# A second gate branch by seven products of quarters, and low parts of weights by accumulating transfers, in a hybrid decoder layer

## The chip, the cores and the metric

The kernel runs on one core of one Trainium2 chip. The metric is the time of one launch on the device in microseconds (us). Three runs of the kernel before gave a median of 1034.51 us (1033.88 to 1037.33). The engines of a core work side by side, each through its own instruction list in order: TensorE (PE) multiplies matrices, VectorE (DVE), ScalarE (ACT) and GpSimd (POOL) work elementwise, SyncE (SP) only issues transfers (DMAs). An instruction that waits holds back everything behind it on its own engine.

## The reference

One pre-norm layer over 512 tokens of width 1024, in float32. A normed input `u` goes through one wide projection `w_in`. Its columns feed three token mixers (attention in three dilated groups, multi-scale pooling, a chunked state space scan) and three gates:

```python
u = rmsnorm(x, ln1_g[i])
proj = u @ w_in[i]
q, k, v, pool_in, z, xbc, dt_raw, gate_pre = jnp.split(proj, split_idx, axis=-1)
...
y_b = pool_mixer(pool_in, pool_w[i], pool_scale[i]) @ w_b[i]
...
gates = jax.nn.sigmoid(gate_pre + b_gate[i]).reshape(b, s, N_BRANCH, D_MODEL)
merged = gates[:, :, 0] * y_a + gates[:, :, 1] * y_b + gates[:, :, 2] * y_c
x = x + merged @ w_o[i]
x = x + conv_ffn(rmsnorm(x, ln2_g[i]), ffn_w_up[i], ffn_conv_w[i], ffn_conv_b[i], ffn_w_down[i])
```

The change concerns `gates[:, :, 1]`, a product of `u` (512 x 1024) with 1024 columns of `w_in`, and how some weights are split.

## The kernel before

**Three products for one.** PE multiplies in a reduced format. Every float32 operand is split into a high part (rounded) and a low part (what rounding left). A product is the sum of three: high x high, high x low, low x high. `uh` and `ul` hold the parts of `u`, transposed, so that the 1024 inputs lie on partitions in 8 blocks of 128. A weight block goes through a `Job`: `fetch` (L184) loads it into `raw` (pool `wraw`, 2 buffers), `cast` (L196) rounds it on ACT into `wh` (3 buffers) in two halves, `lows` (L216) subtracts on DVE into `wl` (2 buffers), and the job's body runs the matmuls (`mm3`, L235) and hands the PSUM tile (pool tag `mm`, 4 buffers) to an evacuation.

**The order of the work** is written out by hand. `program()` yields the jobs in order, and the engine lists of PE, ACT, DVE and POOL are exactly the order in which the instructions are emitted. Before the body of job n the main loop emits `prepare`: the low part of job n+1, the cast of job n+2 (its two halves put off to the next two `step`s), the fetch of job n+3. So on ACT the casts for job n+2 stand behind the evacuations of job n, and the low part of job n+2 comes after both casts. `job.form` makes a weight by a subtraction on DVE at the cast, `job.then` subtracts after the low part. `wraw` has two buffers, so a fetch waits until the low part that reads the buffer's earlier content is done.

**Fillers.** `step()` advances everything in `running` and takes one more item from `waiting`: `attend(g)` queues the attention of one group as items (scores on PE, bias and maximum on DVE, exponentials on ACT, then two steps later transposes on PE, L769), `ssd_prep`, and so on. A job steps once per column chunk. With a chunk in `more` it runs as `chunk_a2`, which does the three products over the first four blocks, steps, and then does the other four.

**Seven products for eight.** `sevens` (L341) and `qk_sevens` (L647) compute a projection as a 2 x 2 block product by 7 products of quarters instead of 8. `sums_of_u` (L400) makes the sums of quarters of `u` that this takes, `side_u` hands them out, and two quarters of the weight wait in `ypool` (tag `xs`, 2 buffers, which later hold the SSD input). In `qk_sevens` a weight quarter of 128 columns is loaded into PE and 256 tokens of `u` move through it.

**Around the change** the order before is: `pool_out_job`; `branch_jobs(1, w_b, ...)`, 4 jobs of two column chunks that make `MG`, with the attention of group 0 as filler; the gates of the second branch, chunks 0 to 3 (`gate_jobs(1, 0, SPLIT)`, L1146); seven jobs for the values of groups 1 and 2 (`v_pair`); seven for the queries and keys of group 1; `attend(1)`; gate chunks 4 to 7; 6 jobs of the SSD input (`xbc_evac`, L900 and L904); `ssd_start`. A gate chunk is 24 matmuls of 512 columns. Its evacuation is a sigmoid on ACT and a product with `MG` on DVE (L1148).

Of the kernel before, what the change touches and what calls it, by code (L numbers as in the profile page):

```python
# [10 lines left out]
F32 = mybir.dt.float32  # L11
F32R = mybir.dt.float32r
AF = mybir.ActivationFunctionType
OP = mybir.AluOpType
# [58 lines left out]
class Job:  # L73


    def __init__(self, parts, k, c, body):
        self.parts, self.k, self.c, self.body = parts, k, c, body
        self.raw = self.split = None
        self.late = self.short = False
        self.load = self.form = self.then = None  # L80


@with_exitstack
def trunk(ctx: ExitStack, tc, out, x, rel_bias, ln1_g, w_in, b_gate, w_a, pool_w, pool_scale, w_b,
# [80 lines left out]
    def after(n, it):  # L165
        for _ in range(n):
            yield
        yield from it
# [40 lines left out]
    def lows(job, cuts=1, eng=None):  # L209

        w, h = job.c // cuts, job.high
        l = wlp.tile([P, job.k, job.c], F32R, name="wl", tag="wl")
        job.split = h, l
        for i in range(cuts):
            o = slice(i * w, (i + 1) * w)
            (eng or dve).tensor_tensor(l[:, :, o], job.raw[:, :, o], h[:, :, o].bitcast(F32),  # L216
                                       OP.subtract)
            yield

    def low(job, cuts=1, eng=None):  # L220
        for _ in lows(job, cuts, eng):
            pass
        if job.then:
            job.then()

# [174 lines left out]
    def sums_of_u(p):  # L400

        f = []
        for k in (2 * p, 2 * p + 1):
            f.append(T("uf"))
            dve.tensor_tensor(f[-1], uh[:, k, :].bitcast(F32), ul[:, k, :].bitcast(F32), OP.add)
        yield
        yield from sums_of(*f, T("sah", F32R), T("sal", F32R),
                           lambda j, h, l: US.__setitem__((j, p), (h, l)))
# [733 lines left out]
    def gate_jobs(b, lo=0, hi=8):  # L1142
# [6 lines left out]

        return jobs_a(w_in, C_GATE + b * D + lo * P, hi - lo, uhk, ulk, KD, evac)  # L1150

    def branch_jobs(b, w, parts, nk, last=False, more=()):
        def evac(m, ps):
            if b == 1:
                MG[m] = T("yo")
                act.copy(MG[m], ps)
                return
            s = SG[b, m]
            dve.tensor_tensor(s, s, ps, OP.mult)
            (dve if last else pool).tensor_tensor(MG[m], MG[m], s, OP.add)  # L1160
            if last:
                h, l = T("mgh", F32R), T("mgl", F32R)
                act.copy(h, MG[m])
                dve.tensor_sub(l, MG[m], h.bitcast(F32))
                MH[m] = (h, l)

        return jobs_a(w, 0, 8, lambda k: parts[k][0], lambda k: parts[k][1], nk, evac,
                      width=256 if nk > 4 else 512, more=more)
# [273 lines left out]
    def program():  # L1442
# [4 lines left out]
        yield from pool_out_job()  # L1447
        yield Call(lambda: attend(0))
        yield Call(lambda: waiting.insert(3, ssd_prep()))
        for i, job in enumerate(branch_jobs(1, w_b, YB, 8, more=range(7))):  # L1450
            if i == 3:
                yield Call(lambda: running.extend(after(p, sums_of_u(p)) for p in range(4)))
            yield job
        load, pair = v_pair()
        yield Call(load)
        yield from gate_jobs(1, 0, SPLIT)
        loads, qk = qk_sevens(1)
        for i, job in enumerate(pair):
            yield job
            if i == 4:  # L1460
                yield Call(loads)
        yield from qk
        yield Call(lambda: attend(1))
        yield from gate_jobs(1, SPLIT)
        yield from jobs_a(w_in, C_XBC, 12, uhk, ulk, KD, xbc_evac)
        yield Call(ssd_start)
        yield from qk_jobs(2)
        yield Call(lambda: attend(2))
# [215 lines left out]
NBIG = 54  # L1684
MORE = 2
AT = ((9, 10, 11, 12, 13, 14, 15), (17, 17, 18, 19, 20, 21, 22))
SPLIT = 4
MIX = "ZZ0zz1ggggaa"
SSD_ORDER = ((0, 0, 1), (1, 0, 1), (0, 1, 1), (2, 0, 1), (1, 1, 1), (3, 0, 1), (2, 1, 1), (3, 1, 1))
WARM = 12  # L1690
# [29 lines left out]
```

## Time and profile before

| what | value |
|---|---|
| median of 3 runs | 1034.51 us |
| time of the profiled execution | 1034.33 us |
| its span in the profile | 1032.0 us |
| PE busy | 99% of the span |
| ACT, DVE, POOL busy | 48%, 69%, 13% |
| mean granted clock of TensorE | 0.999 |

What lies outside the span is 1034.33 - 1032.0 = 2.3 us. A sum that is made on the span is carried to the time of the run with that difference unchanged. In the views below, a row of the timeline gives start, length, engine, line, operation, output <- input and count. A row of the groups gives count, busy time, mean ns of one, and the idle time before it with what ended it.

### The profile page before, as it was taken

Reading aid. Unit: us, or ns where it says so; the run is one execution under the profiler, and the core shown is the slowest. Engines: PE = TensorE matmul, PEld = TensorE weight load, DVE = VectorE, ACT = ScalarE, POOL = GpSimd, SP = SyncE. Lnnn points to the kernel's source line nnn. Section 1 sums busy time; section 2 is a strip of 40 time slices with the busy share of each in tenths; the row PEclk is TensorE's granted clock in tenths of the full one; section 3 lists DMA queues with packets and bytes.
Section 4 is the critical chain, followed back from the end, with each engine's and each line's share of the span. In section 5 each row is a group of like instructions: output and inputs, shape, how many; then the busy total and the mean of one; then the engine's idle time right before and its main releaser. Section 6 shows DMA issues by size and latency. Waiting matters only on the chain.

```text
span 1032.0 us, 13285 instructions
## 1 busy us (share of the span) xinstructions
PE 1021.4 (99%) x5276; PEld 858.8 (83%) x5276; DVE 714.3 (69%) x948; ACT 498.7 (48%) x800; POOL 133.5 (13%) x114
## 2 busy tenths in 40 slices
PE   9999999999999999999999999999999999999997
PEld 8998877899888887788888888898888888888885
DVE  6553566788756648666688856767778759876776
ACT  6432545454674363567575324545445544445334
POOL 1770000000000001100044501101111100111002
PEclk9999999999999999999999999999999999999999
DMA  8444312134322364551253625543231233412222
GB/s 256 148 128 139 107 57 75 31 88 137 123 82 82 94 155 110 132 144 45 79 157 121 202 82 205 175 143 114 82 123 41 85 119 98 148 41 82 82 82 82
DMA packets 112300, 115.52 MB, mean 112 GB/s; under 512 B 5203, under 2 KB 97174, under 8 KB 112239
## 3 DMA queue, kind: packets, MB, share of 16 engines
q1 hardware_dynamic: 111647, 113.83, 36.1%
q8 instruction: 41, 0.67, 0.3%
q10 hardware_dynamic: 592, 0.86, 0.2%
q14 instruction: 20, 0.16, 0.0%
HBM read 110.87 MB, written 2.22 MB: 110 GB/s over the span
## 4 chain that ended last, share of the span: by engine, by line
PE 90%; DVE 5%; ACT 3%; issue 1%; DMA 1%; ACTq 0%; DVEq 0%
PE pa L235 30%; PE pu L235 22%; PE pb L235 12%; PE pd L235 7%; PE pqk L235 6%; PE pa L1571 2%; PE pq L235 2%; PE pu L1375 1%; PE ps L740 1%; PE pt L769 1%; PE ppw L235 1%; PE po L781 1%; DVE wl L216 1%; DVE xs L1130 1%; PE py L1054 1%
## 5 line engine op out<-in xcount | busy, mean ns | idle before, releaser
L216 DVE TENSOR_TENSOR wl<-raw,wh 128x2048 fp32r<-128x2048 f32 (+3 forms) x93 | 213.5, 2297 | 47.8 <-ACT wh L196 42.7
L196 ACT CAST wh<-raw 128x1024 fp32r<-128x1024 f32 (+3 forms) x184 | 183.6, 1017 | 40.9 <-DMA raw<-in_ffn_w_down_dram 13.2
L1248 DVE SCALAR_TENSOR_TENSOR hc<-pu,fcol,hc 128x510 f32<-128x510 f32 x88 | 65.8, 748 | 48.4 <-ACT hc L1245 46.8
L235 PE MATMUL pa<-uh,wh 128*128 128x512 f32 x384 | 98.4, 398 | 0.0
L235 PE MATMUL pa<-ul,wh 128*128 128x512 f32 x384 | 94.9, 389 | 0.0
L235 PE MATMUL pa<-uh,wl 128*128 128x512 f32 x384 | 94.8, 389 | 0.0
L235 PEld LDWEIGHTS pa<-ul,wh 128*128 128x128 f32 x384 | 72.1, 188 | 15.1
L235 PEld LDWEIGHTS pa<-uh,wl 128*128 128x128 f32 x384 | 72.1, 188 | 15.0
L235 PE MATMUL pu<-uh,wh 128*128 128x512 f32 (+1 forms) x352 | 83.6, 379 | 0.0
L235 PE MATMUL pu<-uh,wl 128*128 128x512 f32 (+1 forms) x352 | 83.5, 379 | 0.0
L235 PE MATMUL pu<-ul,wh 128*128 128x512 f32 (+1 forms) x352 | 83.5, 379 | 0.0
L235 PEld LDWEIGHTS pa<-uh,wh 128*128 128x128 f32 x384 | 70.4, 188 | 14.8 <-issue 1.0
L235 PEld LDWEIGHTS pu<-ul,wh 128*128 128x128 f32 x352 | 64.2, 188 | 12.5
L235 PEld LDWEIGHTS pu<-uh,wl 128*128 128x128 f32 x352 | 64.2, 188 | 12.5
L235 PEld LDWEIGHTS pu<-uh,wh 128*128 128x128 f32 x352 | 64.1, 188 | 12.4
L1245 ACT ACTIVATE hc<-pu,fcol,fcol 128x512 f32<-128x512 f32 x40 | 31.2, 780 | 79.7 <-PE pu L235 79.7
L1253 POOL TENSOR_TENSOR hc<-hc 128x512 f32<-128x512 f32 x22 | 31.7, 1442 | 288.6 <-DVE hc L1248 253.6
L1022 POOL TENSOR_TENSOR xd<-xc,dtz 128x512 f32<-128x512 f32 x6 | 6.4, 1062 | 356.1 <-issue 307.7
L762 ACT ACTIVATE sb<-sb,nmls 128x128 f32<-128x128 f32 (+1 forms) x72 | 30.1, 419 | 30.4 <-DVE nmls L759 17.7
L1146 ACT ACTIVATE sg<-pa,col 128x512 f32<-128x512 f32 x24 | 16.5, 687 | 45.0 <-PE pa L235 44.9
L1250 ACT ACTIVATE hc<-hc 128x512 f32<-128x512 f32 x22 | 13.9, 632 | 41.0 <-DVE hc L1248 41.0
L216 DVE TENSOR_TENSOR wl<-w,wh 128x2048 fp32r<-128x2048 f32 (+1 forms) x14 | 29.9, 2135 | 5.3 <-ACT wh L196 5.3
(379 smaller groups left out, 1891.0 us busy)
## 6 DMA issues: line engine op xcount, KB each, us to landing
raw<-in_w_in_dram SPq DMA_DIRECT2D x25, 1024.0 KB, 5.4
raw<-in_ffn_w_up_dram SPq DMA_DIRECT2D x22, 1024.0 KB, 5.2
raw<-in_w_o_dram SPq DMA_DIRECT2D x8, 1024.0 KB, 6.5
raw<-in_w_in_dram SPq DMA_DIRECT2D x14, 512.0 KB, 3.9
raw<-in_ffn_w_down_dram SPq DMA_DIRECT2D x6, 1024.0 KB, 5.2
raw<-in_w_in_dram SPq DMA_DIRECT2D x6, 768.0 KB
raw<-in_w_b_dram SPq DMA_DIRECT2D x4, 1024.0 KB, 5.0
al<-ad SPq DMA_DIRECT2D x16, 256.0 KB, 7.1
```

Of the source, the lines that this page charges most:

```text
L196: act.copy(job.high[:, :, o], job.raw[:, :, o])
L216: (eng or dve).tensor_tensor(l[:, :, o], job.raw[:, :, o], h[:, :, o].bitcast(F32), OP.subtract)
L235: pe.matmul(ps, l, r, start=first and n == 0, stop=last and n == total - 1)
L740: pe.matmul(pss[i][:, o:o + w * P], q[r, n * P:(n + 1) * P], k[r, kb * P:(kb + w) * P], start=True, stop=True)
L762: act.activation(sb[:, off:off + w * P], sb[:, off:off + w * P], AF.Exp, bias=nm[:, n, h:h + 1], accum_out=ls[:, n, h:h + 1])
L769: pe.transpose(pt[:, o:o + P], sb[:, o:o + P], eye)
L1146: act.activation(s, ps, AF.Sigmoid, bias=col[:, o:o + 1])
L1245: act.activation(t, ps, AF.Identity, bias=ff["c1"][:, ff["b"] + m:ff["b"] + m + 1], scale=fw(2, m))
L1248: dve.scalar_tensor_tensor(t[:, sh:], ps[:, :S - sh], fw(k, m), t[:, sh:], OP.mult, OP.add)
L1250: act.activation(t, t, AF.Silu)
L1253: pool.tensor_tensor(a, a, t, OP.mult)
L1571: pe.matmul(first[2 * n + j][:, lo:hi], a[:, k, j * P:(j + 1) * P], b[:, k, lo:hi], start=a is wh and b is uh and k == 0, stop=a is wl and ...
```

## The change

The gates of the second branch leave `gate_jobs` and become `gate_sevens(1)`, seven jobs after the queries and keys of group 1: each takes a quarter of the weight (4 blocks of 128 inputs by 512 columns) and moves 256 tokens through each of its 16 blocks, 48 matmuls a job. Within a job all products with the high parts of two column blocks come before those with the low part. The sigmoids run on 256 columns each. `attend(1)` comes after them, so its items fill the SSD input jobs, 10 of whose 12 chunks now step in the middle. The sums of `u` start two jobs earlier, one every two steps, and all 8 chunks of `branch_jobs(1)` step in the middle.

Where `job.moved` is set, the low part of those blocks isn't made by DVE: ACT writes `-raw`, rounded, into `wl`, and POOL issues a transfer that adds `raw` to it in place, in pieces of 4 blocks at most. `moved` is 8 of 8 blocks for the 4 jobs of `branch_jobs(1)` and the 6 of the SSD input, and 2 of 4 for the 7 gate jobs: 8 + 12 + 7 = 27 such transfers of 128 x 1024 numbers. No other job is changed.

```diff
--- before.py
+++ after.py
@@ -77,6 +77,7 @@
         self.parts, self.k, self.c, self.body = parts, k, c, body
         self.raw = self.split = None
         self.late = self.short = False
+        self.moved = 0
         self.load = self.form = self.then = None
 
 
@@ -218,8 +219,21 @@
             yield
 
     def low(job, cuts=1, eng=None):
-        for _ in lows(job, cuts, eng):
-            pass
+        if job.moved:
+            l, at = wlp.tile([P, job.k, job.c], F32R, name="wl", tag="wl"), job.k - job.moved
+            job.split = job.high, l
+            for k in range(at, job.k, 4):
+                o = slice(k, min(k + 4, job.k))
+                act.mul(l[:, o, :], job.raw[:, o, :], -1.0)
+                pool.dma_start(l[:, o, :].bitcast(F32), job.raw[:, o, :], accum_op=OP.add)
+            if at:
+                dve.tensor_tensor(l[:, :at, :], job.raw[:, :at, :], job.high[:, :at, :].bitcast(F32),
+                                  OP.subtract)
+        else:
+            for _ in lows(job, cuts, eng):
+                pass
         if job.then:
             job.then()
 
@@ -1149,6 +1163,97 @@
 
         return jobs_a(w_in, C_GATE + b * D + lo * P, hi - lo, uhk, ulk, KD, evac)
 
+    def gate_sevens(b):
+        W = []
+        c = C_GATE + b * D
+        quarter = lambda two, h: w_in[:, c + S * h:c + S * h + S].rearrange(
+            "(k two p) c -> two p k c", two=2, p=P)[two]
+        r1, r2, r5, r7 = {}, {}, {}, {}
+        def load():
+            for two in (1, 0):
+                W.append(ypool.tile([P, 4, S], F32, name="w3", tag="xs"))
+                sp.dma_start(W[-1], quarter(two, 1))
+        def job(j, raw, form, use):
+            def body(ws):
+                wh, wl = ws
+                parts = side_u(j)
+                pss = [MM("pg") for _ in range(2)]
+                for n in range(2):
+                    for low_ in range(2):
+                        for i in range(2):
+                            ps = pss[i][:, 256 * n:256 * n + 256]
+                            o = slice((2 * i + n) * P, (2 * i + n + 1) * P)
+                            for a, part in ((wl, 0),) if low_ else ((wh, 0), (wh, 1)):
+                                for k in range(4):
+                                    pe.matmul(ps, a[:, k, o], parts[k][part],
+                                              start=a is wh and part == 0 and k == 0,
+                                              stop=a is wl and k == 3)
+                for i in range(2):
+                    use(i, pss[i])
+                step()
+            new = Job([raw] if raw is not None else [], 4, S, body)
+            new.form = form
+            new.moved = MOVED
+            if raw is None:
+                new.load = lambda: None
+            return new
+        def keep(r):
+            def use(i, ps):
+                r[i] = T("rg")
+                act.copy(r[i], ps)
+            return use
+        def emit(right, hi, i, a, ps):
+            t = T("sg")
+            dve.tensor_tensor(t, a, ps, OP.add)
+            def rest():
+                for n in range(2):
+                    m = 4 * right + 2 * i + n
+                    h, o = t[:, 256 * n:256 * n + 256], col[:, o_bg + 8 * b + m:o_bg + 8 * b + m + 1]
+                    act.activation(h, h, AF.Sigmoid, bias=o)
+                yield
+                for n in range(2):
+                    y = MG[4 * right + 2 * i + n][:, 256 * hi:256 * hi + 256]
+                    dve.tensor_tensor(y, y, t[:, 256 * n:256 * n + 256], OP.mult)
+            running.append(rest())
+        def p5(i, ps):
+            keep(r5)(i, ps)
+            dve.tensor_tensor(r2[i], r2[i], ps, OP.add)
+        def p6(i, ps):
+            dve.tensor_tensor(r1[i], r1[i], ps, OP.add)
+            dve.tensor_tensor(r7[i], r7[i], r1[i], OP.add)
+            emit(1, 0, i, r1[i], r2[i])
+            if i:
+                for i in range(2):
+                    emit(1, 1, i, r7[i], r5[i])
+        one = job("A11", quarter(0, 0), None, keep(r1))
+        two = job("A12", quarter(1, 0), None, lambda i, ps: emit(0, 0, i, r1[i], ps))
+        three = job(4, None, lambda: W[0], keep(r2))
+        four = job(3, None, lambda: W[1], keep(r7))
+        five = job(1, None, lambda: one.raw, p5)
+        six = job(2, None, lambda: W[0], p6)
+        last = job("A22", None, lambda: diff(two.raw, two.raw, W[0]),
+                   lambda i, ps: emit(0, 1, i, r7[i], ps))
+        def then():
+            diff(one.raw, W[1], one.raw)
+            diff(W[1], W[0], W[1])
+        three.then = then
+        five.then = lambda: diff(W[0], W[0], one.raw)
+        return load, [one, two, three, four, five, six, last]
     def branch_jobs(b, w, parts, nk, last=False, more=()):
         def evac(m, ps):
             if b == 1:
@@ -1447,22 +1552,29 @@
         yield from pool_out_job()
         yield Call(lambda: attend(0))
         yield Call(lambda: waiting.insert(3, ssd_prep()))
-        for i, job in enumerate(branch_jobs(1, w_b, YB, 8, more=range(7))):
-            if i == 3:
-                yield Call(lambda: running.extend(after(p, sums_of_u(p)) for p in range(4)))
+        for i, job in enumerate(branch_jobs(1, w_b, YB, 8, more=range(8))):
+            if i == 1:
+                yield Call(lambda: running.extend(after(2 * p, sums_of_u(p)) for p in range(4)))
+            job.moved = MOVED_B
             yield job
-        load, pair = v_pair()
-        yield Call(load)
-        yield from gate_jobs(1, 0, SPLIT)
+            if i == 1:
+                load, pair = v_pair()
+                yield Call(load)
         loads, qk = qk_sevens(1)
         for i, job in enumerate(pair):
             yield job
             if i == 4:
                 yield Call(loads)
-        yield from qk
+        loads, gates = gate_sevens(1)
+        for i, job in enumerate(qk):
+            yield job
+            if i == 4:
+                yield Call(loads)
+        yield from gates
         yield Call(lambda: attend(1))
-        yield from gate_jobs(1, SPLIT)
-        yield from jobs_a(w_in, C_XBC, 12, uhk, ulk, KD, xbc_evac)
+        for job in jobs_a(w_in, C_XBC, 12, uhk, ulk, KD, xbc_evac, more=range(10)):
+            job.moved = MOVED_X
+            yield job
         yield Call(ssd_start)
         yield from qk_jobs(2)
         yield Call(lambda: attend(2))
@@ -1684,7 +1796,7 @@
 NBIG = 54
 MORE = 2
 AT = ((9, 10, 11, 12, 13, 14, 15), (17, 17, 18, 19, 20, 21, 22))
-SPLIT = 4
+MOVED, MOVED_B, MOVED_X = 2, 8, 8
 MIX = "ZZ0zz1ggggaa"
 SSD_ORDER = ((0, 0, 1), (1, 0, 1), (0, 1, 1), (2, 0, 1), (1, 1, 1), (3, 0, 1), (2, 1, 1), (3, 1, 1))
 WARM = 12
```

## The prediction

> **What bounds the kernel.** I read the page first, then who waits for whom on PE, then PE's timeline around the change. The page's first part and the shares of its chain, and the one wait of PE in this stretch (us in total, times, longest):
>
> ```profile
> PE 1021.4 (99%) x5276; PEld 858.8 (83%) x5276; DVE 714.3 (69%) x948; ACT 498.7 (48%) x800; POOL 133.5 (13%) x114
> ...
> PE 90%; DVE 5%; ACT 3%; issue 1%; DMA 1%; ACTq 0%; DVEq 0%
> ```
>
> ```profile
> PE pq L235 <- DVE wl L216: 0.3, 1, 0.3
> ```
>
> PE is the bound: busy 99%, and in the jobs beside the change it waits 0.3 us, once, for a low part of weights. So a matmul taken away is worth its time, and any new wait of PE costs its full length: no later idle time of PE can pay it back.
>
> PE's timeline (start, length) gives the pace of its two matmul forms and two points in time that I need:
>
> ```profile
> 195.38 1.98 PE L235 MATMUL pa<-uh,wh 128*128 128x512 f32 x8
> 197.19 1.98 PE L235 MATMUL pa<-ul,wh 128*128 128x512 f32 x8
> ...
> 235.40 0.64 PE L235 MATMUL pq<-uh,wh 128*128 128x256 f32 x4
> 235.88 0.64 PE L235 MATMUL pq<-ul,wh 128*128 128x256 f32 x4
> ...
> 261.60 0.64 PE L235 MATMUL pq<-uh,wh 128*128 128x256 f32 x4
> ...
> 266.45 2.00 PE L235 MATMUL pa<-uh,wh 128*128 128x512 f32 x8
> ```
>
> From start to start, 512 moving columns take 1.81 / 8 = 0.2266 us, 256 take 0.48 / 4 = 0.120 us. A half costs more than half. The last of the query and key jobs starts at 261.60 and ends at 266.45; there the new gate jobs begin.
>
> **Part 1, the matmuls.** Removed: 8 chunks x 24 = 192 matmuls x 0.2266 = 43.5 us. Added: 7 jobs x 48 = 336 x 0.120 = 40.3 us, 5.76 us a job. The sum is **-3.2 us**, not the eighth (5.4 us) that seven for eight suggests. Attention, sums of `u` and the other jobs keep their matmuls, only moved.
>
> **Part 2, the time of an accumulating transfer, D.** I call D the time from the end of ACT's `-raw` to the low part that PE may read. No transfer of POOL and none that adds is in this trace. The nearest rows are (KB each, median us from issue to landing):
>
> ```profile
> raw<-in_w_in_dram SPq DMA_DIRECT2D x25, 1024.0 KB, 5.4
> raw<-in_w_in_dram SPq DMA_DIRECT2D x14, 512.0 KB, 3.9
> al<-ad SPq DMA_DIRECT2D x16, 256.0 KB, 7.1
> out_dram<-xg SPq DMA_DIRECT2D x7, 256.0 KB, 2.3
> ```
>
> The transfer writes 512 KB (row: 3.9) but must read that and its 512 KB destination, 1024 KB (row: 5.4). I take the middle of these two nearest rows, **D = 4.6 us**, and keep 2.3 and 7.1 as ends. [...]
>
> DVE's share of this part is a gain that buys nothing: 10 whole and 7 half low parts leave it, but it bounds no stage. ACT's added pass matters where ACT is in the chain.
>
> **Part 3, the chain of the gate jobs.** ACT's timeline beside the change, then groups of ACT and of DVE (count | busy us, mean ns | idle before):
>
> ```profile
> 258.55 3.47 ACT L196 CAST wh<-raw 128x768 fp32r<-128x768 f32 x4 [3.55 <-DVE raw L338]
> ...
> 268.76 2.00 ACT L196 CAST wh<-raw 128x1024 fp32r<-128x1024 f32 x2 [6.74 <-DMA raw<-in_w_in_dram]
> ...
> 275.62 0.40 ACT L762 ACTIVATE sb<-sb,nmls 128x128 f32<-128x128 f32 x1
> ...
> 277.29 1.28 ACT L1146 ACT_TABLE_LOAD   x1
> ```
>
> ```profile
> L762 ACT ACTIVATE sb<-sb,nmls 128x256 f32<-128x256 f32 x18 | 9.1, 505 | 20.9 <-DVE nmls L751 12.6 <-DVE nmls L759 8.3
> ...
> L682 ACT COPY rq<-pq 128x512 f32<-128x512 f32 x3 | 1.8, 585 | 4.2 <-PE pq L235 4.2
> ```
>
> ```profile
> L1159 DVE TENSOR_TENSOR sg<-sg,pa 128x512 f32<-128x512 f32 x16 | 10.6, 682 | 12.8 <-PE pa L235 12.7
> ...
> L338 DVE TENSOR_TENSOR w<-w,w 128x2048 f32<-128x2048 f32 x2 | 4.6, 2293 | 0.1
> ```
>
> A cast of 128x1024, and so the `-raw` pass of that size, takes 1.0 us back to back; two copies out of PSUM 1.1; a sigmoid on 256 columns 0.4 (0.505 less the overlap); a table load 1.28; a subtraction on 2048 columns 2.25; an addition on 512 columns 0.6 to 0.7. In a gate job the first low part that comes from a transfer is read after 18 matmuls, 18 x 0.12 = 2.16 us, and 30 (3.6 us) follow. The order on ACT for the low part of job n+1 is: evacuation of job n-1, both casts of n+1, `-raw`. It can't be earlier, since the buffer of `wl` comes free when job n-1 ends. Then D. I name the seven jobs by number.
>
> - **Job 1.** Casts end at 262.0, `-raw` at 263.0, landing 267.6, needed 266.45 + 2.16 = 268.6. No wait.
> - **Job 2.** Its `raw` can't land earlier than the load that the second row shows at 268.76, since it waits for the same buffer and, on SP, stands behind the two quarters kept aside (1024 KB each), whose buffers come free earlier. Casts to 270.8, `-raw` 271.8, landing 276.4. Job 2 starts at 266.45 + 5.76 = 272.2 and needs it at 274.4: **wait 2.0**, end at 276.4 + 3.6 = 280.0.
> - **Job 3.** After job 1 ends: copies 273.3, casts 275.3, `-raw` 276.3, landing 280.9, needed 282.2. No wait; end 285.8.
> - **Job 4.** Its weight is a difference. DVE makes job 3's half low part (276.4), then two subtractions (280.9), and only then the two additions of job 2 (282.2). ACT: first cast 281.9, table load 283.2, four sigmoids that stand ahead of the second cast 284.8, second cast 285.8, `-raw` 286.8, landing 291.4, needed 287.9: **wait 3.5**, end 295.0.
> - **Jobs 5, 6, 7.** Job 5 has its part at 295.5, before 297.2. Job 6: copies of job 4 to 296.1, casts 298.1, `-raw` 299.1, landing 303.7, needed 303.0: **wait 0.7**, end 307.3. Job 7 lands when needed, 309.5; end 313.1.
>
> **Part 4, the first SSD input job.** Its second cast and its two `-raw` passes stand on ACT behind eight sigmoids, whose eight additions on DVE need job 6's results: 307.0 + 8 x 0.6 = 311.8, sigmoids 312.7, cast 313.7, `-raw` 314.8 and 315.8. The chunk steps in the middle, so PE wants the first half of the low part after 8 matmuls, 313.1 + 1.8 = 314.9. It lands at 314.8 + 4.6 = 319.4: **wait 4.5**. Behind it on PE stands all of the attention's work.
>
> The second wait there is hidden one step further. Now the row of SP's waits, and PE's rows for an attention item:
>
> ```profile
> SPq L184 <- DVE wl L216: 754.9, 76, 32.8
> ```
>
> ```profile
> 284.21 1.16 PE L740 MATMUL ps<-k,q 64*128 64x128 f32 x16
> 285.30 0.66 PE L769 MATMUL pt<-eye,sb 128*128 128x128 f32 x4
> ```
>
> A load waits until the low part has read its buffer. That reader is now the transfer, so the weights of the third SSD job are issued at 315.8 + 4.6 = 320.4 and land 5.4 later, at 325.8. Their cast stands on ACT ahead of the first exponentials: 326.8, table load 328.1, four exponentials of 0.4 329.8. PE wants these for the transposes two steps after the first scores: 319.4 + 4 x 0.2266 + 1.1 + 24 x 0.2266 + 1.1 = 327.9. **Wait 1.9.** The later SSD jobs last over 10.9 us each, more than chain and D together.
>
> **Sum.** -3.2 + 2.0 + 3.5 + 0.7 + 4.5 + 1.9 = +9.4. On the profiled execution, 1034.3 + 9.4 = 1043.7; it stands 0.2 under the median of the runs. I say **1044 us**. With D = 2.3 the waits are 0, 3.1, 0, 2.2 and 1.9, net +4.0, 1038.3. With D = 7.1 each comes later: 1.5 (job 1), 3.0, 5.1, 3.3, 7.0 and 1.9, net +18.6, 1052.9. In `branch_jobs(1)` I cost the transfers at nothing: a job there lasts over 10.9 us plus attention, and the low part has from the job's start until 1.8 us into the next. That cover is gone from D of about 8 on.
>
> **Rivals.**
> - **The waits are hidden: faster.** If ACT's order hinders less than I drew and D is short, only the matmuls count: 1034.3 - 3.2 = 1031.1. For it speaks that PE waited 0.3 us in all beside the query and key jobs, which have the same form of chain. Against it: there, a low part has no D, and casts are three quarters as long. It decides at the sum of the waits: the part of job 4 would have to land at 286 instead of 291, and that of the first SSD job within 0.1 us of `-raw`, while even the row of 256 KB takes 2.3.
> - **The transfers are much slower: slower still.** If POOL issues them slowly or the adding halves the rate, D passes 7.1 and the SSD jobs and `branch_jobs(1)` wait too: 1053 and more. POOL's rows for one form speak for some of this:
>
> ```profile
> L1160 POOL TENSOR_TENSOR yo<-yo,sg 128x512 f32<-128x512 f32 x8 | 14.6, 1854 | 21.7 <-DVE sg L1159 21.7
> ...
> L1039 POOL TENSOR_TENSOR st<-st,dts 128x512 f32<-128x512 f32 x4 | 4.2, 1041 | 22.1 <-PE py L1054 11.2 <-ACT wh L196 11.0
> ```
>
>   The same size takes 1.04 or 1.85 us. [...]
> - **The change doesn't save matmul time.** If the moving of halves ran at 0.135 us in place of 0.120, 336 matmuls would cost 45.4 and the sum would be +1.9 before any wait. With the waits this is 1049. Row against it: 0.120 holds over all 252 matmuls of the query and key jobs.
> - **Between.** Waits and gain cancel: 1031.4 to 1037.6.
>
> **Chances.** Forecast with D between 2.3 and 7.1: 0.62. Hidden waits: 0.15. Slow transfers: 0.08. Slow halves: 0.04, mostly inside the range too. Between: 0.11. The range goes from the hidden case, 1031, to D = 7.1, 1053, and leaves out the slow transfers and half of the hidden case. A change of 0.3%, 3.1 us, is about what a measurement of this kernel can tell from none: faster 0.15, same 0.11, slower 0.74.
>
> **What would show it.** In the profile after: `pg` matmuls 0.12 us apart; PE idle for `wl` in gate jobs 2, 4 and 6 but not in 3, 5 and 7; the longest wait in the first SSD input job; a wait of `pt` on the exponentials behind the cast of a late `raw`. Wrong would be: low parts landing under 2 us after `-raw`, or no idle time of PE between the gate jobs.

## The result, and the profile after

| | before | after |
|---|---|---|
| median of the runs, us | 1034.84 (1033.88 to 1037.33) | 1068.98 (1068.52 to 1070.65) |
| ratio | | 1.0332, interval 1.0315 to 1.0349 |
| profiled execution: span, us | 1032.0 | 1066.7 |
| mean granted clock of TensorE | 0.999 | 0.987 |

The change makes the kernel 34 us slower. I had said 10 us slower, and about 18 at the upper end of the range.

The page of after, PE's part and the shares of its chain:

```profile
PE 1031.3 (97%) x5420; PEld 871.2 (82%) x5420; DVE 710.5 (67%) x967; ACT 526.8 (49%) x843; POOL 157.2 (15%) x141
...
PE 80%; DVE 8%; ACT 6%; DMA 4%; issue 3%; ACTq 0%; POOL 0%; DVEq 0%; POOLq 0%; SPq 0%
```

PE's share of the chain falls from 90% to 80%, and yet PE is busy 10 us longer, for less work: that is a first sign of slow matmuls. Who PE waits for between 110 and 400 us (us in total, times, longest); before had 0.3 us here:

```profile
PE pa L249 <- DMA wl<-raw: 5.4, 1, 5.4
PE pg L1193 <- DMA wl<-w: 5.4, 3, 4.1
PE po L795 <- ACT sb L784: 5.2, 2, 2.7
PE pt L783 <- ACT sb L776: 4.4, 2, 3.7
PE pg L1193 <- DMA wl<-raw: 2.8, 1, 2.8
```

More than half of it (13.6 us) is for low parts from transfers, most of the rest (9.6) for attention's probabilities on ACT. PE's timeline (start, length, and in brackets the idle time before) shows the waits and what follows them:

```profile
254.69 1.65 PE L1193 MATMUL pg<-uh,wl 128*128 128x256 f32 x6 [2.82 <-DMA wl<-raw]
256.13 1.05 PE L1193 MATMUL pg<-uh,wh 128*128 128x256 f32 x4
256.99 1.05 PE L1193 MATMUL pg<-ul,wh 128*128 128x256 f32 x4
...
259.88 0.64 PE L1193 MATMUL pg<-uh,wh 128*128 128x256 f32 x4
260.36 0.64 PE L1193 MATMUL pg<-ul,wh 128*128 128x256 f32 x4
...
279.39 1.65 PE L1193 MATMUL pg<-sbh,wl 128*128 128x256 f32 x6 [4.13 <-DMA wl<-w]
280.84 1.05 PE L1193 MATMUL pg<-sbh,wh 128*128 128x256 f32 x4
...
311.36 2.08 PE L249 MATMUL pa<-uh,wl 128*128 128x512 f32 x4 [5.39 <-DMA wl<-raw]
...
326.24 1.63 PE L783 MATMUL pt<-eye,sb 128*128 128x128 f32 x4 [3.69 <-ACT sb L776]
```

Four matmuls of a half take 0.48 us from start to start at 259.88, 0.120 each as forecast, but 0.86 at 256.13: 0.215 each, for 3 to 6 us behind each long wait. Each slice of 10 us in which this happens has a lower granted clock (0.83 at 250, 0.73 at 280, 0.69 at 310; rows below).

**Where the 34.7 us of span come from.** From 110 to 430 us PE waits for 24.3 us (before 0.6): +23.7. The granted clock is 0.50 in five stretches of 3.41 or 6.83 us (from 162.57, 254.73, 278.62, 309.34 and 326.41 us). PE is busy for 21.1 us of them, and half of that is lost: +10.5 (before none while PE works). The matmuls saved: -3.2. That makes 31.0. Of the other 3.7, 2.6 are busy time of PE beyond these terms (it is busy 9.9 us longer in all) and 1.1 are idle time elsewhere; no run here takes these apart. By place: the group 2 query and key products start at 398.57 us, 34.6 later than the 363.99 of before; what follows takes 668 us in both.

### The profile page after: what moved, and what is told of

The parts are those of the page before. It is cut to its first block, busy times and chain, and to the rows that moved or that the text cites. A ratio compares the mean times of both kernels' runs of the same rounds, so it can differ in the third digit from the quotient of the medians.

```text
span 1066.7 us, 13744 instructions
## 1 busy us (share of the span) xinstructions
PE 1031.3 (97%) x5420; PEld 871.2 (82%) x5420; DVE 710.5 (67%) x967; ACT 526.8 (49%) x843; POOL 157.2 (15%) x141
## 3 DMA queue, kind: packets, MB, share of 16 engines
q1 hardware_dynamic: 109599, 113.83, 34.6%
q0 software_dynamic: 3888, 14.16, 7.0%
## 4 chain that ended last, share of the span: by engine, by line
PE 80%; DVE 8%; ACT 6%; DMA 4%; issue 3%; ACTq 0%; POOL 0%; DVEq 0%; POOLq 0%; SPq 0%
PE pu L249 21%; PE pa L249 21%; PE pb L249 11%; PE pd L249 7%; PE pqk L249 6%; PE pa L1683 2%; PE pq L249 2%; ACT wh L197 1%; PE pg L1193 1%; DMA wl<-raw 1%; PE pu L1480 1%; PE ppw L249 1%; PE po L795 1%; DVE wl L217 1%; DMA raw<-in_w_in_dram 1%
## 5 line engine op out<-in xcount | busy, mean ns | idle before, releaser
L217 DVE TENSOR_TENSOR wl<-raw,wh 128x2048 fp32r<-128x2048 f32 (+3 forms) x79 | 181.5, 2299 | 44.7 <-ACT wh L197 42.8
L249 PE MATMUL pa<-uh,wl 128*128 128x512 f32 x320 | 81.7, 393 | 5.4 <-DMA wl<-raw 5.4
L249 PE MATMUL pa<-uh,wh 128*128 128x512 f32 x320 | 85.1, 403 | 0.0
L249 PE MATMUL pa<-ul,wh 128*128 128x512 f32 x320 | 81.0, 390 | 0.0
L249 PEld LDWEIGHTS pa<-uh,wl 128*128 128x128 f32 x320 | 60.5, 189 | 18.4 <-DMA wl<-raw 5.8
L249 PEld LDWEIGHTS pu<-uh,wl 128*128 128x128 f32 x352 | 64.2, 188 | 12.4
L249 PEld LDWEIGHTS pu<-uh,wh 128*128 128x128 f32 x352 | 64.1, 188 | 12.4
L249 PEld LDWEIGHTS pa<-ul,wh 128*128 128x128 f32 x320 | 60.4, 189 | 12.9
L249 PEld LDWEIGHTS pa<-uh,wh 128*128 128x128 f32 x320 | 59.4, 191 | 12.5 <-issue 1.2
L230 POOL DMA_DIRECT2D wl<-raw x24 | 21.0, 881 | 257.1 <-ACT wl L229 222.6
L918 DVE SCALAR_TENSOR_TENSOR xs<-pa,col,xs 128x509 f32<-128x509 f32 (+2 forms) x24 | 18.0, 749 | 33.1 <-ACT xs L914 32.6
L197 ACT CAST wh<-w 128x1024 fp32r<-128x1024 f32 (+1 forms) x34 | 32.4, 973 | 10.0 <-DVE w L352 7.4
```

The lines of the kernel that those rows point to most:

```text
L197: act.copy(job.high[:, :, o], job.raw[:, :, o])
L230: pool.dma_start(l[:, o, :].bitcast(F32), job.raw[:, o, :], accum_op=OP.add)
L249: pe.matmul(ps, l, r, start=first and n == 0, stop=last and n == total - 1)
L918: dve.scalar_tensor_tensor(t[:, sh:], ps[:, :S - sh], col[:, o_cw + 12 * k + m:o_cw + 12 * k + m + 1], t[:, sh:], OP.mult, OP.add)
```

## Experiments

Each row of a table is against the kernel before on the same chip. MOVED, MOVED_B and MOVED_X say how many blocks of 128 inputs of a gate, branch and SSD input job (of 4, 8 and 8) have their low part by transfers. "PE idle" is what PE waited for from 110 to 430 us; it and the clock are of the profiled execution. On these chips the kernel before took 1033.9 to 1034.9 us, so a difference between rows of two tables is good to about 1 us.

### The transfers taken away, stage by stage

```diff
-MOVED, MOVED_B, MOVED_X = 2, 8, 8
+MOVED, MOVED_B, MOVED_X = 0, 0, 0    # e1_none; e2_gates 2,0,0; e3_branch 0,8,0; e4_ssd 0,0,8
```

> The changed kernel with all 27 accumulating transfers taken back: every low part by DVE, the seven gate products and the new order kept. Theory A (PE waits for low parts that come by transfer, and after each longer wait its clock is lower for some us): the 24 us of waits and the 14 us of slow matmuls go, the 3.2 us of fewer matmul time stay, 1031 to 1036 us. Rival B (the order of the gate jobs itself, differences and sigmoids ahead of a cast, makes PE wait whoever makes the low part): 1045 us and more, with waits of PE for wl by DVE in gate job 4 and the first SSD input job. Rival C (the sums of u and attention in their new places cause the waits): about 1055 us.

> Transfers kept only in the seven gate jobs (2 of 4 blocks). Theory A: the gate stretch stays at about 54 us as in the changed kernel (14 over 40.3), the other stretches as without transfers: some 12 to 14 us above e1_none. Rival B: no more than 3 us above e1_none.

> Transfers kept only in the four jobs of the second branch. Theory A in the form of the prediction (low parts land in time there) would give e1_none exactly; the trace of the changed kernel shows a wait of 2.5 us for a copy that stands on ACT behind two passes of -raw, so now: 3 to 5 us above e1_none, with PE waiting for ACT and not for a transfer. Rival C: as e1_none, since the sums of u stay where they are in both.

> Transfers kept only in the six SSD input jobs. Theory A: the wait for the first low part (4 to 5 us) and the waits of the attention behind the late load (about 7 us), with slow matmuls after them: 15 to 19 us above e1_none. Rival C: within 5 us of e1_none, since the attention runs in these jobs in both.

| kernel | us, median | ratio to before, interval | PE idle 110-430 us | clock |
|---|---|---|---|---|
| e1_none | 1050.23 | 1.0146 (1.0131 to 1.0162) | 12.4 | 0.994 |
| e2_gates | 1056.45 | 1.0203 (1.0186 to 1.0220) | 16.5 | 0.993 |
| e3_branch | 1050.78 | 1.0157 (1.0130 to 1.0183) | 13.5 | 0.992 |
| e4_ssd | 1061.90 | 1.0260 (1.0243 to 1.0277) | 19.1 | 0.989 |

The transfers explain 18.7 of the 34 us: 6 in the gates, 12 in the SSD inputs, next to nothing in the branch (whose runs spread from 1049.0 to 1054.6). The gates and the SSD inputs came out between their two recorded cases, the branch below the 3 to 5 us that I expected. The larger surprise is e1_none: **without one transfer the new order is still 15 us slower.** Its PE timeline in the gates:

```profile
270.31 0.74 PE L1193 MATMUL pg<-sbh,wh 128*128 128x256 f32 x4 [2.05 <-ACT wh L197]
...
272.64 2.07 PE L1193 MATMUL pg<-sbh,wl 128*128 128x256 f32 x8 [0.93 <-DVE wl L217]
```

and ACT's at that point:

```profile
265.25 1.06 ACT L197 CAST wh<-w 128x1024 fp32r<-128x1024 f32 x1 [6.94 <-DVE w L352]
266.32 1.28 ACT L1221 ACT_TABLE_LOAD   x1
267.62 1.71 ACT L1221 ACTIVATE sg<-sg,col 128x256 f32<-128x256 f32 x4
269.23 1.03 ACT L197 CAST wh<-w 128x1024 fp32r<-128x1024 f32 x1
```

This is job 4 as the prediction drew it: the first cast waits for DVE's difference, and a table load and four sigmoids stand ahead of the second. No transfer is needed for PE to wait there.

### What in the order costs: sigmoids, close steps, seven products

```diff
# e5_late, on e1_none
-            running.append(rest())
+            running.append(after(1, rest()))
# e6_steps, on e1_none
-        for job in jobs_a(w_in, C_XBC, 12, uhk, ulk, KD, xbc_evac, more=range(10)):
+        for job in jobs_a(w_in, C_XBC, 12, uhk, ulk, KD, xbc_evac):
# e7_whole, on e1_none (and without the load of the quarters)
-        yield from gates
+        yield from gate_jobs(1)
```

> The changed kernel without any accumulating transfer (e1_none), and the sigmoids of the gates start one step later than now. Theory: in e1_none the second cast of gate job 4 and the first casts of the SSD inputs stand behind sigmoids on ACT, and this makes PE's waits of 2.05 + 0.93 us at job 4 and 2.06 us at the first SSD job, and the two half-clock windows behind them (together about 5 us lost); with the sigmoids out of the way most of that goes: 1038 to 1044 us. Rival: the waits come from DVE's differences or from the order of the loads, and the sigmoids only happen to stand there: 1049 to 1051, as e1_none.

> e1_none with the SSD inputs' matmuls in one piece of 24 again (a step of attention after each, none in the middle, as the kernel before had it). Theory: the steps in the middle crowd attention's scores, exponentials and transposes together and let PE come to the low part after 8 matmuls instead of 16, and so cause the waits pt 1.32, po 1.25 and a good part of the 2.06 us at the first SSD job, with a half-clock window: 1043 to 1047 us. Rival: those waits come from what stands behind the gates on ACT and DVE, whatever the steps: 1049 to 1052; and attention that is late by ten steps is then waited for later.

> e1_none with the second branch's gates as whole products (the four jobs of 1.5 x 32 matmuls of 0.2266 us each that the kernel before had), all of them behind the query/key products; the rest of the new order stays. Theory A, the seven products cost more in waits than they save: matmuls +3.2 us, waits of job 4 (2.98) and the first SSD job (2.06) gone with two half-clock windows (about 5): 1043 us, 1041 to 1046. Theory B, the seven products are worth their 3.2 us and the loss lies in the rest of the order: 1051 to 1055.

| kernel | us, median | ratio to before, interval | PE idle | clock |
|---|---|---|---|---|
| e5_late | 1050.2 | 1.0153 (1.0138 to 1.0168) | 10.2 | 0.993 |
| e6_steps | 1042.49 | 1.0083 (1.0068 to 1.0098) | 7.6 | 0.993 |
| e7_whole | 1039.96 | 1.0055 (1.0039 to 1.0072) | 5.1 | 0.998 |

e5_late missed its number, though not its mechanism. Its waits in the gates and at the first SSD input job (250 to 300 us):

```profile
PE pg L1193 <- DVE wl L217: 1.6, 3, 0.6
PE pa L249 <- DVE wl L217: 1.3, 1, 1.3
```

The 2.05 us for the cast are gone, and the gates take 42.8 us (251.25 to 294.05) instead of 46.3. But they start 1.4 us later, the SSD inputs take 86.0 instead of 84.5 us, and the query and key products of group 2 start at 380.03 instead of 380.71. The granted clock of the profiled executions tells where the gain went. In e5_late it is at half from 162.56 us, behind a wait of 2.25 us that e1_none has too (2.27) without that, and for two stretches of 3.41 us in the SSD inputs (from 309.34 and 316.17) where e1_none has one (from 301.90). Each costs 1.7 us. What was won in the gates was lost in slow matmuls behind other waits; that another engine than PE bounds the SSD inputs is not shown by this run.

In e6_steps, with the steps of attention as far apart as before, 7.7 us go. e7_whole gives up the 3.2 us of matmuls and is still about 10 us faster than e1_none: in this order **the seven products, with the differences, sigmoids and loads that they bring, lose some 13 us in waits and clock to save 3.2**. Both came out below their ranges, by 0.5 and 1 us.

### Is it the idle time that slows the matmuls?

Into the changed kernel, products that nobody reads go in front of three waits (DUMMY = 18 in gate job 1, 28 in job 4, 20 in the first SSD input job, where `chunk_a2` gets them in the same way; the diff shows the gate jobs alone):

```diff
+                        if low_ and n == 0 and j in DUMMY:
+                            other = SM("pd")
+                            for q in range(DUMMY[j]):
+                                pe.matmul(other[:, :256], wh[:, 0, :P], uh[:, 0, :256],
+                                          start=True, stop=True)
```

> The changed kernel whole, with products nobody reads put in front of three of PE's waits: 18 of 0.12 us (2.2 us) in gate job 1, 28 (3.4 us) in gate job 4, 20 of 0.2266 us (4.5 us) in the first SSD job; each is a little shorter than the wait it stands in (2.82, 4.13, 5.39 us). Theory: it is the idle time that makes the granted clock fall, and the matmuls after each wait run at half speed for that; PE then gets 10 us more work and the kernel is yet faster: the slow matmuls behind these three waits (about 8 us) go, 1059 to 1063 us. Rival: the matmuls run slowly there for another reason (the transfers that move at that time, ports, operands): 1068 to 1071, no faster.

e8_busy took 1068.63 us, ratio 1.0334 (1.0314 to 1.0353): no faster. Three slices of 10 us of after, then of e8_busy (slice, length, busy us of PE, PEld, DVE, ACT and POOL with their instructions, granted clock, DMA share, GB/s):

```profile
250.00:260.00 10.00, 7.18 (x47) 6.97 (x46) 2.77 (x4) 3.35 (x4) 0.86 (x1) 0.83 0.68 141
280.00:290.00 10.00, 10.00 (x65) 10.00 (x65) 2.25 (x3) 4.03 (x5) 0.22 (x1) 0.73 0.61 157
310.00:320.00 10.00, 8.64 (x39) 6.80 (x40) 1.63 (x3) 2.63 (x3) 1.75 (x2) 0.69 1.02 186
```

```profile
250.00:260.00 10.00, 7.66 (x65) 7.46 (x64) 1.38 (x2) 4.56 (x6) 0.86 (x1) 1.00 0.55 109
280.00:290.00 10.00, 9.94 (x83) 9.74 (x82) 4.71 (x4) 6.52 (x9) 0.86 (x1) 1.00 0.76 184
310.00:320.00 10.00, 7.80 (x56) 6.25 (x56) 1.38 (x2) 0.02 (x1) 1.22 (x2) 1.00 1.02 229
```

The clock column answers the question: where PE was kept busy the clock stays at 1.00, so idle time is what lowers it. The time answers another question. From the first gate product to attention's first transposes the changed kernel takes 76.7 us (249.55 to 326.24), 7.1 of them lost to half clock. e8_busy loses none there and still takes 75.5 us (248.16 to 323.63), since other waits grew: PE reads the first SSD low part at 308.75 instead of 311.36, but then the transposes wait for 5.83 us instead of 3.69. So in this stretch **the slow matmuls mostly fill time in which the next part was not ready anyway**; what PE waits for there comes from ACT, the loads and the transfers. Behind it the clock falls in e8_busy as well, after the waits of 5.83 and 2.74 us. That costs 5.5 us, against 1.7 in the changed kernel, and group 2 begins at 398.80, as in after (398.57). This second part is partly chance (see the last section).

### The easings together, and the same transfers in other orders

e9_three takes e5_late and e6_steps together and moves one more thing:

```diff
-        yield Call(lambda: waiting.insert(3, ssd_prep()))
+        yield Call(lambda: waiting.insert(0, ssd_prep()))
```

e10_after_steps is the edit of e6_steps on the changed kernel; e11_half is the changed kernel with `MOVED_X = 4`; e12_before_ssd is the kernel before with the changed `low` and this alone:

```diff
-        yield from jobs_a(w_in, C_XBC, 12, uhk, ulk, KD, xbc_evac)
+        for job in jobs_a(w_in, C_XBC, 12, uhk, ulk, KD, xbc_evac):
+            job.moved = 8
+            yield job
```

> e1_none (no accumulating transfers) with three things put back or loosened: the SSD inputs' matmuls in pieces of 24, the gates' sigmoids a step later, and the preparation of the SSD's decays at the head of attention's queue instead of three items later, so that its steps do not fall on the first sums of u. Theory: the losses are separate and each is a stretch in which DVE and ACT are too full: 1042.5 (e6_steps) less 2 to 3 for the gates and less 2 to 3 for the branch, 1036 to 1039 us. Rival: what is won ahead of the SSD inputs is waited for there again, as with the late sigmoids alone: 1041 to 1044.

> The changed kernel with all its transfers, only the SSD inputs' matmuls in pieces of 24 again. Theory: the low part is then wanted after 16 matmuls instead of 8 and attention's items stand further apart, so most of what the SSD inputs lose goes, that of the transfers too: 1052 to 1058 us. Rival: a raw buffer that is held until its transfers have read it, and so a late next load, sets the pace whatever the steps are: 1061 or more (the 8 us that the same edit brought without transfers, at most).

> The changed kernel with one transfer of four quarters of k per SSD input job instead of two; DVE subtracts the other half. Theory: what counts is when the last transfer lands, and two of them on one queue land later than one: about half of the 12 us that the SSD transfers cost is gone, 1061 to 1064 us. Rival: the fixed time of any transfer, together with the buffer that it holds, is the cost, and half the bytes save next to nothing: 1066 to 1069.

> The kernel before, in its own order, with the low parts of the six SSD input jobs by accumulating transfers and nothing else of the change. Theory A: load, two passes on ACT, transfers and the freeing of the raw buffer are a loop through two buffers that is longer than a job's 10.9 us of matmuls, so the transfers cost by themselves: 1040 to 1046 us. Theory B: they cost only where attention's items stand close and the gates' work is in the way; in the old order they are covered: 1033 to 1037.

| kernel | us, median | ratio to before, interval | PE idle | clock |
|---|---|---|---|---|
| e9_three | 1037.47 | 1.0029 (1.0019 to 1.0038) | 6.0 | 0.998 |
| e10_after_steps | 1061.16 | 1.0255 (1.0239 to 1.0270) | 18.7 | 0.989 |
| e11_half | 1067.42 | 1.0316 (1.0275 to 1.0357) | 22.7 | 0.986 |
| e12_before_ssd | 1033.85 | 0.9994 (0.9985 to 1.0004) | 0.3 | 0.999 |

e9_three is 12.8 us faster than e1_none, where e5_late alone brings nothing and e6_steps 7.7. The third move was not tried alone, so it is open how the other 5 us divide. In e10_after_steps the same pieces of 24 bring 7.8 us with all transfers in, and no more: the transfers' 18.7 us stay. Half the transferred bytes per SSD job (e11_half) save nothing that can be told.

e12_before_ssd is the sharpest of the runs. Twelve transfers of the same size, and the one wait of PE between 110 and 400 us is the one that was there before:

```profile
PE pq L249 <- DVE wl L217: 0.3, 1, 0.3
```

although from issue to landing they take longer than in the changed kernel (there 4.5/4.7/8.2):

```profile
DMA to landing us min/median/max: 4.6/6.6/9.8
```

So in the old order neither a slow transfer nor the raw buffer that it holds costs anything. There, every job in front lasts 10.9 us of matmuls; in the new order the seven gate jobs in front last 5.76.

### The border, and long jobs in front

e13_but_first is the changed kernel, e14_three_but_first e9_three with `MOVED_X = 8`, both with

```diff
-            job.moved = MOVED_X
+            job.moved = MOVED_X if i else 0
```

e15_three_all is e9_three with `MOVED_X = 8` for all six; e16_prep1 is e14_three_but_first with `waiting.insert(1, ssd_prep())`; e17_whole_moved is e7_whole, e18_three_moved e9_three, each with the transfers of the changed kernel (2, 8, 8; in e17_whole_moved the gates are whole products and have none).

> The changed kernel with the first SSD input job's low part by DVE; all the other transfers stay. Theory: the SSD transfers cost only at the border, where the last gate job (5.8 us of matmuls) is all that the first of them has as cover, and what follows is the echo of that wait: most of the 12 us of e4_ssd over e1_none goes, 1057 to 1060 us. Rival: each transfer keeps its raw buffer from the next load, so the five others cost as much as before: 1064 to 1069.

> e9_three with the low parts of the SSD input jobs by transfers, all but the first. Theory of the border: nothing waits for them, and DVE gets 11 us free: 1035 to 1037.5 us, the same as e9_three or a little less. Rival, the loop through the raw buffers: 1040 to 1045.

> e9_three with the low parts of all six SSD input jobs by transfers; against e14_three_but_first only the first job differs. Theory of the border: PE waits about 4 us for the first of them and the matmuls behind it run at half clock for a window: 1042 to 1047 us, so 5 to 10 us above e14_three_but_first. Rival, the loop: 1042 to 1047 too, but within 2 us of e14_three_but_first.

> e14_three_but_first with the preparation of the SSD's decays one item later, to take away the wait of 1.1 us for its transposes that e9_three has at about 145 us and keep the 2.3 us of the branch. Hoped for: the best of the new order, 1033 to 1036 us, level with the kernel before. Rival: the preparation then meets the first sums of u again: 1036 to 1039.

> The changed kernel with the transfers of the branch and of the SSD inputs, but the second branch's gates as four jobs of whole products (10.9 us of matmuls each) instead of seven of 5.8 us; against e7_whole (1040.0) only the transfers are added. Theory: it is the short jobs of the gates in front that leave the first SSD transfers no cover; behind long jobs they are covered as in the old order, 1038 to 1044 us. Rival: the transfers cost 10 us or more in the SSD inputs wherever attention's items stand close: 1049 to 1053.

> The changed kernel with all its transfers and the three easings of e9_three. If costs add: e15_three_all (1041.5) plus the 6 us that the gates' transfers cost (e2_gates over e1_none) and nothing for the branch, 1046 to 1049 us. Rival, waits and transfers make each other worse: 1053 to 1058, so that the easings bring no more here than the 8 us of the pieces of 24.

| kernel | us, median | ratio to before, interval | PE idle | clock |
|---|---|---|---|---|
| e13_but_first | 1060.05 | 1.0248 (1.0232 to 1.0265) | 16.7 | 0.990 |
| e14_three_but_first | 1040.81 | 1.0075 (1.0054 to 1.0095) | 6.3 | 0.997 |
| e15_three_all | 1041.49 | 1.0070 (1.0053 to 1.0086) | 7.2 | 0.997 |
| e16_prep1 | 1041.29 | 1.0070 (1.0055 to 1.0085) | 5.8 | 0.997 |
| e17_whole_moved | 1045.6 | 1.0097 (1.0080 to 1.0114) | 6.2 | 0.993 |
| e18_three_moved | 1051.56 | 1.0170 (1.0142 to 1.0198) | 14.3 | 0.996 |

In the changed kernel the first SSD job's transfers alone are worth 8.9 us (e13_but_first), in the eased order nothing: e14 and e15 agree within their intervals. There, PE waits 0.32 and 1.26 us for the two of the first job instead of 5.39: the sigmoids no longer stand ahead of them, and the low part is wanted after 16 matmuls instead of 8. The transfers of the later jobs still cost 3 to 4 us. In e14 PE waits three times for them (1.56, 1.35 and 0.43 us), but other waits have gone, so that all waits make 6.3 us against the 6.0 of e9_three; half clock from 321.71 us adds 1.7. Both times fit the recorded rival, the loop through the raw buffers, within 0.5 us. That this loop is the mechanism is not shown, since in e12_before_ssd it costs nothing. So the border is not a price of its own; it goes when the sigmoids and the close steps go, with the short gate jobs still in front. e16_prep1 gained nothing and came out above both its cases. In e17_whole_moved, with long gate jobs in front and the close steps left in, PE waits for no transferred low part at all; its waits over 0.5 us are these two:

```profile
162.65 1.97 PE L795 MATMUL po<-sb,v 128*64 128x128 f32 x14 [2.51 <-ACT sb L784]
...
323.51 1.97 PE L795 MATMUL po<-sb,vr 128*64 128x128 f32 x14 [2.74 <-ACT sb L784]
```

Still it is 5.6 us above e7_whole, between its two cases. ACT with its added passes is later with attention's copies (the second wait is 1.1 us in e7_whole), and half clock follows both waits: these 14 take 1.97 us, the same ones at 162.51 us in e1_none 1.09. In the profiled execution half clock costs 4.6 us, in that of e7_whole nothing. e18_three_moved came out between its two cases. In its gates the transfers are waited for in five jobs, 0.5 to 2.8 us each, longest in the first:

```profile
252.86 0.98 PE L1193 MATMUL pg<-uh,wl 128*128 128x256 f32 x6 [2.80 <-DMA wl<-raw]
...
288.81 1.53 PE L1193 MATMUL pg<-sah,wl 128*128 128x256 f32 x6 [2.32 <-DMA wl<-w]
```

**The way from after back to before**: 1069.0; the three easings 1051.6 (-17.4); gates' and branch's transfers out 1041.5 (-10.1); the SSD's out 1037.5 (-4.0); what is left is 3.0, in which the seven products' -3.2 is already counted. Another sequence gives other steps (e1_none first: -18.7), since waits and transfers make each other worse. No kernel of the new order beat the old one; e12_before_ssd equals it.

## Why the prediction was wrong, step by step

- **"Any new wait of PE costs its full length", since "PE is the bound"**: this step failed first, in both directions. A wait can cost more than its length, because the matmuls behind it may run at 0.215 us for 3 to 6 us; the sum had no term for the 10.5 us of clock. And PE's time need not be the kernel's: in e8_busy 7.1 us of slow matmuls went, and the stretch up to the transposes became 1.2 us shorter. Where one wait follows another, PE does not bound the stretch.
- **Part 1, matmuls**: 0.120 us held wherever the clock was full, and -3.2 us with it: in e9_three PE is busy for 1018.5 us, before for 1021.4. Attention and sums "only moved" was wrong: the move, and the chain of the new jobs, is what costs. This is the largest failed step. Without transfers the sum had -3.2 us, and e1_none measured +15.3; some 7 of that are the close steps of attention in the SSD inputs. For the waits that the transfers bring the sum had 12.6, and they cost 18.7.
- **Part 2, D**: right in the middle, wrong at the edge. Job 4's low part came 279.39 - 274.40 = 5.0 us after its `-raw`, the first SSD job's 311.36 - 306.3 = 5.1; forecast 4.6. But job 1's took 254.69 - 246.08 = 8.6, beside the load of the next `raw`, issued at 246.06, and outside the 2.3 to 7.1 that I kept. The rows of after from issue to landing (KB each, median us), loads and transfers:

```profile
raw<-in_w_in_dram SPq DMA_DIRECT2D x23, 1024.0 KB, 6.3
...
wl<-raw POOLq DMA_DIRECT2D x24, 512.0 KB, 5.1
...
wl<-w POOLq DMA_DIRECT2D x3, 512.0 KB, 4.5
```

  None of them took less than 4.5 us. That the adding also reads its 512 KB destination, and so goes by the row of 1024 KB, was an assumption of mine that no run shows: the packets of the 27 transfers come to 14.16 MB (queue q0 of after), 512 KB each.
- **Part 3, gate jobs**: job 4, 4.13 for 3.5, and job 6, 0.69 for 0.7, by the mechanisms drawn. Job 2 was forecast to wait 2.0 and did not; job 1 waited 2.82 instead, because of its D, and so gave job 2 its time. Their sum, 8.2 us with job 3, stands against 6.2. What failed is the cost of each: the gates took 54.4 us: 40.3, 8.4 idle (with 0.2 for a cast), and 5.7 more, of which half clock explains 4.7.
- **Part 4, SSD inputs**: right in place and mechanism, 5.39 for 4.5 and 3.69 for 1.9. ACT in after:

```profile
301.90 2.51 ACT L1221 ACTIVATE sg<-sg,col 128x256 f32<-128x256 f32 x6 [1.01 <-DVE sg L1215]
304.32 1.04 ACT L197 CAST wh<-raw 128x1024 fp32r<-128x1024 f32 x1
305.26 2.00 ACT L229 ACTIVATE wl<-raw 128x1024 fp32r<-128x1024 f32 x2
...
323.33 1.04 ACT L197 CAST wh<-raw 128x1024 fp32r<-128x1024 f32 x1 [10.70 <-DMA raw<-in_w_in_dram]
324.40 1.28 ACT L776 ACT_TABLE_LOAD   x1
```

  Sigmoids ahead of cast and `-raw`; then ACT idle for 10.70 us until the late `raw` lands, and the exponentials behind its cast. SP's waits tell the same (us, times, longest; before 754.9 for DVE alone): the loads now wait for the transfers that read the buffer.

```profile
SPq L185 <- DVE wl L217: 600.9, 64, 30.4
SPq L185 <- DMA wl<-raw: 195.8, 14, 36.7
```

  "The later SSD jobs last over 10.9 us each, more than chain and D together" was too simple: attention's waits for ACT (po 2.74 at 348.66 us) follow there too.
- **"In `branch_jobs(1)` I cost the transfers at nothing"**: true of the transfers (e3_branch), false of the stage. The sums of `u`, started two jobs earlier, meet the preparation of the SSD's decays on DVE and ACT, and PE waits 2.2 to 2.6 us at 162 us in every kernel that has both there. With the preparation moved ahead (e14_three_but_first) this wait is gone and one of 1.1 us at 145 takes its place. I had asked of this stage only what the transfers would do.
- **The rivals**: that the waits are hidden failed. "The transfers are much slower", with 1053 and more, came nearest in time, for another reason than the one given. Slow issue on POOL is not seen: it is busy 0.86 to 1.04 us with each transfer (after, L230).

What stays open: how much of e9_three's last 3 us is the branch and how much the gates, and why the gates' transfers cost 6 us with one base and about 10, with the branch's, on another. What the changed kernel costs beside waits and half clock, 3.7 us, is not explained.

## What to carry to other kernels

An algorithm that saves an eighth of a stage's products also makes its jobs shorter (here 5.76 us of matmuls for 10.9), and it is the length of the job in front that hides casts, differences and transfers (behind jobs of 10.9 us PE waited for no transferred low part in e12_before_ssd and e17_whole_moved): weigh the saved matmuls against the cover that is lost. Before an order is changed, ask of every stage that is moved, not only of the new instructions, which engine's queue it now meets. And where an edit wins time in one stage, look at the start of the next ones and at the clock: the win may go in a wait or in slow matmuls there, as the 3.5 us of e5_late in the gates did (46.3 to 42.8) at 1050.2 us for 1050.23.

## What was unexpected of the hardware

- **Idle time of PE of 2 to 3 us can halve the speed of the matmuls behind it, and whether it does depends on where it falls.** After 2.82 us (after, 254.69) a half takes 0.215 us instead of 0.120 for about 3.4 us; after 2.80 us in e18_three_moved (252.86) the next matmuls ran at full speed. In each of the 12 traces with more than one half-clock stretch while PE works, these begin whole multiples of 3.413 us apart (the five of after 27, 7, 9 and 5 times), and all last one, two or three times as long. Here are intervals of that grid in after, then in e18_three_moved (interval, length, busy us and instructions of each engine, granted clock, DMA share, GB/s):

  ```profile
  251.32:254.73 3.41, 0.59 (x6) 0.39 (x4) 0.65 (x2) 2.45 (x3) 0.00 (x0) 1.00 0.75 154
  254.73:258.14 3.41, 3.41 (x16) 3.41 (x17) 0.80 (x1) 0.50 (x1) 0.86 (x1) 0.50 0.40 74
  ```

  ```profile
  248.01:251.43 3.42, 2.06 (x18) 1.85 (x16) 1.74 (x4) 0.99 (x2) 0.00 (x0) 1.00 1.05 235
  251.43:254.84 3.41, 1.98 (x16) 1.98 (x17) 1.23 (x1) 1.96 (x3) 0.86 (x1) 1.00 0.19 37
  ...
  285.56:288.97 3.41, 1.09 (x9) 0.88 (x9) 1.46 (x2) 3.41 (x5) 0.76 (x1) 1.00 0.68 137
  288.97:292.39 3.42, 3.42 (x17) 3.42 (x18) 0.00 (x0) 0.72 (x1) 0.11 (x1) 0.50 0.81 153
  ```

  In after the idle time lies in one interval, and the next one is at half clock. In e18_three_moved the 2.80 us are shared by two intervals and the clock holds, while 2.32 us within one bring it down. Counted so over the 16 traces that have half clock while PE works: behind an interval at full clock with PE busy for less than 1.6 us it was always half (33 times), with more than 2.3 us never, in between either; from half it went back to full behind 2.9 us or more, and never behind 2.81 or less. The grid lies differently in each trace, so which of a kernel's waits brings the clock down is partly chance. This is a count over the traces of this case; no run was made to try it.
- An accumulating transfer of 512 KB within the chip's own buffers took 4.5 to 9.8 us from issue to landing, and the longer ones, in the old order, cost nothing (e12_before_ssd: median 6.6 us in flight, 1033.85 us).
